# Conditioning of gates and second norm in a decoder layer: loads one visit ahead, products of a visit in one run

## The chip, the core and the metric

One core of a Trainium2 chip runs the whole program. The metric is the device time of one execution in microseconds (us), the median of the runs. TensorE is called PE, VectorE DVE, ScalarE ACT, GpSimd POOL and SyncE SP; SP does no arithmetic here, its queue issues most DMAs.

## The reference, cut to what matters

One layer of a hybrid autoregressive decoder, for two request groups with shared weights: a prompt of 256 positions and 8 sequences of 4 positions. N = 288 columns of activations run through every projection; the model width is 2048. Nine condition vectors (one for the prompt, eight for the sequences) give the six modulation vectors of the layer.

```python
mod = silu(c) @ w_ada + b_ada                      # 9 x 12288
sh1, sc1, g1, sh2, sc2, g2 = split(mod, 6)         # parts 0 to 5
h = rmsnorm(x, norm1) * (1 + sc1) + sh1
u_pool, z, xbc, dt = split(h @ w_in)
mix = concat([pool_mixer(u_pool), ssd_mixer(z, xbc, dt)]) @ w_out
x = x + g1 * mix                                   # needs part 2
h2 = rmsnorm(x, norm2) * (1 + sc2) + sh2           # needs parts 3 and 4
gate, val = split(h2 @ w_up)
x = x + g2 * ((silu(conv(gate)) * val) @ w_down)   # needs part 5
y = rmsnorm(x, norm_f)
```

The mixers are a causal pooling mixer (512 columns) and a chunked state-space scan (1536 columns), whose output is multiplied by silu(z) and normalized. "The gates and the second norm" of the title are parts 2, 3 and 4: the gate `g1` of the first residual and the shift and scale of the second norm. The change touches how these three parts are computed, and nothing of what is computed.

## The kernel before, in words

**Large products.** Every projection is taken in three products per 128 x 128 tile of weights (`mm3`, L299 to 302): the weights and the activations are both split into a high part of type fp32r and a remainder, and high x high, high x remainder and remainder x high are summed in PSUM. Activations have 288 columns. The 128 x 1024 block of weights that one load brings (8 tiles, so 24 products) is split by ACT (the cast into `whi`, L286) and DVE (the remainder `wlo`, L288).

**One ring for all weights.** `load` (L267 is its DMA) takes the next tile `raw` of a ring and issues its DMA of 512 KB on SP's queue. The ring has 8 buffers in the stages below (`RAW1`), one more from the sixth column tile of the output projection on; `whi` and `wlo` have 2 each until then, 4 afterwards. A DMA into a buffer can start once the last reader of that buffer is done. A buffer of projection weights is read by its cast and remainder; a buffer of conditioning weights is read by PE itself, as the moving operand of the products. SP issues in the order of the program's text, and a DMA that waits for its buffer holds up those behind it.

**Stages in order of time**: the modulated norm and the first projection's blocks 0 to 5 (tile `xbc`, parts 0 and 1 of the conditioning woven in between); the last block of that projection (`bi == 6`, 28 column tiles of 4 k each, preceded by the small projection `dt` and its elementwise stage `dt_stage`); the z stage (`uz_units`: the remaining columns for z and the pooling mixer, tiles `mm_uz`); the output projection (`mm_out`, `project_units`); the gated feed-forward (`mm_up`, `mm_gate`, `mm_val`, `mm_down`). The scan's small products run woven into the last block and the z stage.

**Conditioning of parts 2, 3 and 4.** `ada_part_units` makes one part. For each of the 16 k it loads two blocks of 128 x 1024 weights and calls `ada_mm` (its product is L329), which issues two products per block: 128 x 32 conditions against 128 x 512 weights, on four column tiles of PE (`tile_position`), so that four products run side by side. With `AY = 2` the generator pauses after every second k. What lies between two pauses is called a visit here: 2 k, 4 loads, 8 products; 8 visits make a part and 24 the three. After its last k the sum goes through ACT (`ada_sb`), four transposes (`ada_tr`) and four additions of the bias into the table `ada`.

The generators of parts 2, 3 and 4 are chained into `adas`, and the main program pulls visits from it at given rates: one every 4 column tiles of the last `xbc` block (`RA1`), one every 5 steps of two k in the z stage (`RA2`), two behind it (`TA`), one every two column tiles of the output projection and one each from column tile 10 on (`ADA_OUT`), and what is left after column tile 13. Part 5 is a call of its own, `adag2`, with one k a visit, between the output projection and the first gate tiles.

**What sets the order.** Instructions are recorded in the order of the text. On PE, ACT and DVE a scheduler may move them, by readiness and by the engine's work; `tc.high_priority()` lets an instruction go ahead of others that are ready, and `tc.keep_in_program_order(i)` ties an instruction to the one recorded before it. The order is fixed when the program is built: on the chip each engine waits at its next instruction, even if a later one could run. The first stage, up to the first norm, is put in order by `in_order`. In the conditioning of parts 0 and 1 (`ada_group_units`) all products of a visit but the first are tied in this way already, and they are taken from the visit's last load backwards, so that PE waits only once, at the first product.

**Around the change.** In the last block, after the products of `dt`: `late_states` issues three DMAs on SP's queue and one copy on POOL; then `dt_stage` runs on DVE and ACT. At the end of the z stage `y_norm` makes the norm of the scan's output (column sums and a broadcast on PE, the multiplication `zy` at L902 on DVE and POOL), and the operands of the output projection are formed by ACT and DVE (L1062 to 1071).

Of the kernel before, what the change touches and what calls it, by code (L numbers as in the profile page):

```python
# [12 lines left out]
F32 = mybir.dt.float32  # L13
# [5 lines left out]
P = 128  # L19
D = 2048  # L20
KT = D // P
# [30 lines left out]
AY = 2  # L52
# [26 lines left out]
def _xbc_chunks(bi):  # L79
    (k0, gk), (a, b) = BLOCKS[bi]  # L80
    mper = RAWC // (gk * P)
    cuts = [a, *([4, 8] if bi == 0 else []), *range(a + (12 if bi == 0 else mper), b, mper), b]
    return [(list(range(k0, k0 + gk)), list(range(m, n))) for m, n in zip(cuts, cuts[1:])]
# [78 lines left out]
def kernel(ctx: ExitStack, tc, ins, outs):  # L162
    nc = tc.nc
# [6 lines left out]
    pa = ctx.enter_context(tc.tile_pool(name="pa", bufs=1, space=PSUM))  # L170
# [29 lines left out]
    ada = kp.tile([P, 6, KT, NC9], F32, name="ada")  # L200
    amul = kp.tile([P, 2, KT, NC9], F32, name="amul")
    bada = early[:, V_BADA:V_BADA + 96].rearrange("p (a k) -> p a k", a=6)
    sc_c = kp.tile([P, KT, 32], F32, name="sc_c")
# [3 lines left out]
    @contextmanager  # L207
    def in_order(*engines):

        traced = nc.cur_bb.bb.instructions  # L210
        n0 = len(traced)
        yield
        prev = {}
        for i in list(traced[n0:]):
            if i.engine in engines:
                if i.engine in prev:
                    tc.add_manual_dep(i, prev[i.engine].name, mybir.DependencyInfo(
                        mybir.DependencyClass.NoSync, mybir.DependencyReason.DATA), reason="in_order")
                prev[i.engine] = i
# [44 lines left out]
    def load(key):  # L264
        off, cols = S.items[key]
        t = wp[0].tile([P, RAWC], F32, tag="raw", name="raw_" + "_".join(map(str, key)))
        nc.sync.dma_start(t[:, :cols], wflat[off:off + P * cols].rearrange("(p n) -> p n", p=P))  # L267
        return t

    queue = deque(_need_order())  # L270
    ahead = {}
    nloads = [0]

    def top_up():

        while queue and nloads[0] - min((n for n, _ in ahead.values()), default=nloads[0]) < RAW0 + RAW1:
            key = queue.popleft()
            ahead[key] = (nloads[0], load(key))
            nloads[0] += 1

    def fetch(key):
        return ahead.pop(key)[1]

    def split_steps(raw, a, n, name):
        hi = wp[0].tile([P, RAWC], F32R, tag="whi", name="whi_" + name)
        yield nc.scalar.copy(hi[:, :n], raw[:, a:a + n])  # L286
        lo = wp[0].tile([P, RAWC], F32R, tag="wlo", name="wlo_" + name)
        yield hi, lo, nc.vector.tensor_tensor(lo[:, :n], raw[:, a:a + n], hi[:, :n].bitcast(F32), ALU.subtract)  # L288

    def split(raw, a, n, name, urgent=True, pin=False):  # L290
        with tc.high_priority() if urgent else nullcontext():
            cast, (hi, lo, rest) = split_steps(raw, a, n, name)
        if pin:
            tc.keep_in_program_order(cast)
            tc.keep_in_program_order(rest)
        return hi, lo

    def mm3(ps, whi, wlo, c, bh, bl, first, last, n=P):
        w = slice(c * n, c * n + n)  # L299
        nc.tensor.matmul(ps, whi[:, w], bh, start=first, stop=False)  # L300
        nc.tensor.matmul(ps, whi[:, w], bl, start=False, stop=False)  # L301
        nc.tensor.matmul(ps, wlo[:, w], bh, start=False, stop=last)  # L302
# [23 lines left out]
    def ada_mm(ps, raw, k, c0, nb, js):  # L326
        for j in js:
            c = c0 + (j - js[0]) * nb
            nc.tensor.matmul(ps[32 * j:32 * j + 32, :nb], sc_c[:, k, :], raw[:, c:c + nb],  # L329
                             start=(k == 0), stop=(k == KT - 1), tile_position=(0, 32 * j))  # L330

    def ada_sb(ps, nb, name, r=P):
        asb = kp.tile([P, 512], F32, tag="asb", name="asb_" + name)
        nc.scalar.copy(asb[0:r, :nb], ps[0:r, :nb])
        return asb

    def ada_tr(asb, nb, name, r=P):
        pt = aux("adat_" + name)
        for i in range(nb // P):
            nc.tensor.transpose(pt[:, i * r:(i + 1) * r], asb[0:r, i * P:(i + 1) * P], ident[0:r, 0:r])  # L340
        return pt

    def ada_scale(which, part, norm, k0, gk):
        nc.vector.scalar_tensor_tensor(
            out=amul[:, which, k0:k0 + gk, :], in0=ada[:, part, k0:k0 + gk, :], scalar=1.0,
            in1=norm[:, k0:k0 + gk].unsqueeze(2).to_broadcast([P, gk, NC9]),
            op0=ALU.add, op1=ALU.mult)

    def ada_group_units(gi):
# [49 lines left out]
            nc.vector.tensor_tensor(o, src, b.unsqueeze(3).to_broadcast([P, 2, nj // 2, NC9]), ALU.add)  # L399
        ada_scale(0, 1, early[:, V_N1:V_N1 + KT], k0, gk)  # L400

    def ada_part_units(part, ay=1):
        ps = pa.tile([P, 512], F32, tag="ada", name=f"adap{part}")
        for k in range(KT):
            raws = [load(("adap", part, k, h)) for h in range(2)]
            for h in range(2):
                ada_mm(ps, raws[h], k, 0, 512, range(2 * h, 2 * h + 2))
            if k % ay == ay - 1:
                yield
        asb = ada_sb(ps, 512, f"p{part}")  # L410
        yield
        pt = ada_tr(asb, 512, f"p{part}")
        for i in range(4):
            o = ada[:, part].rearrange("p (j i) c -> p j i c", j=4)[:, :, i, :]
            b = bada[:, part].rearrange("p (j i) -> p j i", j=4)[:, :, i]
            src = pt[:, i * P:(i + 1) * P].rearrange("p (j c) -> p j c", j=4)[:, :, 0:NC9]
            nc.vector.tensor_tensor(o, src, b.unsqueeze(2).to_broadcast([P, 4, NC9]), ALU.add)
        if part == 4:
            ada_scale(1, 4, vec[:, V_N2:V_N2 + KT], 0, KT)
        yield  # L420
# [105 lines left out]
    def late_loads():  # L526
        nc.vector.tensor_copy(selr, seli)
        nc.vector.tensor_scalar(csr, vec[:, K_TRI:K_TRI + N], 0.0, None, ALU.mult)

    def late_states():  # L530
        nc.sync.dma_start(poolw, ins["pool_w"])
        n = XT * NB * 3
        st = sx[0].tile([P, n + 4 * NB * 15], F32, name="st")
        nc.sync.dma_start(st, ins["st"])
        stc.append(st[:, 0:n].rearrange("p (g m b l) -> p g m b l", g=4, m=5, b=NB))
        nc.gpsimd.tensor_copy(ups.rearrange("p m b l -> p (m b) l")[:, :, 0:15],
                              st[:, n:].rearrange("p (m l) -> p m l", l=15))
# [369 lines left out]
    def chain(*gens):  # L907
        for gn in gens:
            yield from gn

    adas = chain(*(ada_part_units(p, AY) for p in (2, 3, 4)))
    with in_order(*(e.engine for e in (nc.tensor, nc.scalar, nc.vector))):
        nc.scalar.activation(warm, sc_c[:, 0, 0:1], AF.Sqrt, scale=0.0)
        warm_pe(WU[0])
# [1 line left out]
        for q in range(4):  # L916
# [5 lines left out]
            for i in range(4):  # L922
                nc.tensor.matmul(ssum[32 * i:32 * i + 32, :N], ones[:, 0:32], sq[:, i, :],
                                 start=(q == 0), stop=(q == 3), tile_position=(0, 32 * i))
# [16 lines left out]
        parts = [split_steps(t, 0, len(ms) * P, f"xbc0_{i}") for i, (t, (_, ms)) in  # L941
                 enumerate(zip(first, _xbc_chunks(0)))]
# [47 lines left out]
    def pull(gn, rate):  # L990

        credit[id(gn)] = credit.get(id(gn), 0.0) + rate
        while credit[id(gn)] >= 1:
            credit[id(gn)] -= 1
            next(gn, None)

    nloads[0] = len(first) + KT // 4
    for bi in range(len(BLOCKS)):
        last = bi + 1 == len(BLOCKS)
        top_up()  # L1000
        if last:

            wp[0].drop(w0)
            w0_ctx.close()
            sx[0] = mx_ctx.enter_context(tc.tile_pool(name="sx", bufs=1, reuse_waits="tile"))
            hi, lo = split(load(("dt",)), 0, KT * NH, "dt")
            ps = pm.tile([P, 512], F32, tag="mm", name="mm_dt")
            for k in range(KT):
                mm3(ps[0:NH, :N], hi, lo, k, xhi[0][k], xlo[0][k], k == 0, k == KT - 1, NH)
            late_states()  # L1010
            dt_stage(ps)
        elif bi == 4:
            nc.sync.dma_start(vec, ins["vec"])
        elif bi == 5:
            late_loads()
        for i, m in enumerate(xbc_units(bi)):
            if not last:
                top_up()
                if bi == 0 and i in (3, 7, 13):
                    ci = {3: 2, 7: 3, 13: 4}[i]  # L1020
                    ready["xbc", 0, ci] = split(fetch(("xbc", 0, ci)), 0, len(_xbc_chunks(0)[ci][1]) * P,
                                                f"xbc0_{ci}", pin=True)
                if i in VIS[bi]:
                    next(nxt)
                    top_up()
            else:
                pull(back, 0.5 if m < 20 else RB1) if m >= 9 else None
                pull(adas, RA1 / AY)

    late = {}  # L1030
    n = 0
# [31 lines left out]
    for g in range(4):  # L1063
        for t in range(3):
            k = 4 + 3 * g + t
# [353 lines left out]
```

## Time and profile before

| what | value |
|---|---|
| median of 3 runs | 1358.91 us (1358.83 to 1359.32) |
| span of the profiled execution | 1356.6 us, 2.3 us under the median |
| PE busy | 1343.0 us, 99% |
| DVE, ACT, POOL busy | 810.8 us (60%), 579.2 us (43%), 222.1 us (16%) |
| conditioning parts 2 to 4 on PE | between 195 and 475 us of the span |
| read from memory | 309.78 MB, 236 GB/s over the span with what is written |

The profile shows one execution. Its span is what the engines and queues were seen to do; what lies outside of it (2.3 us against the median) is not in the trace. A row of the timeline has the start, the length, the engine, the line in the code, the operation, the tile written and the tiles read, the shapes and the count. Products of PE overlap: a large product is listed with 0.29 us, and the steps between their starts are shorter. A product of the conditioning counts as two records. "Idle before" names the time in which the engine had nothing running and what ended it. A line such as `PE mm_out L301 <- DVE mixl L1068: 0.4, 1, 0.4` says that PE's product waited for DVE: total us, number of waits, the longest. In the view of the DMA issues the time to landing runs from the moment that the queue has issued the DMA to the last byte's arrival.

### The profile page before, as it was taken

The page shows a single profiled execution, that of the slowest core. Times are in us where ns is not written, and L with a number is a line of the kernel's source. Part 1 is how long each engine was busy: PE and PEld are TensorE (multiplying, and loading weights), DVE is VectorE, ACT ScalarE, POOL GpSimd, SP SyncE. Part 2 cuts the span into 40 slices and gives each one's busy share as a digit, 9 for nine tenths or more (in the row PEclk, how much of TensorE's full clock was granted, in tenths as well). Part 3 has the DMA queues.
Part 4 walks back from the last instruction along what each step waited for, and adds up shares of the span by engine and source line. Part 5 has one row for each costly group of instructions (what it writes and reads, how often), then busy time and mean ns, then how long its engine had stood idle before and what let it go on. Part 6 is the DMA issues. An engine that isn't in the chain of part 4 may idle for free.

```text
span 1356.6 us, 26243 instructions
## 1 busy us (share of the span) xinstructions
PE 1343.0 (99%) x10557; PEld 1247.6 (92%) x10557; DVE 810.8 (60%) x1349; ACT 579.2 (43%) x910; POOL 222.1 (16%) x433
## 2 busy tenths in 40 slices
PE   9999999999999999999999999999999999999997
PEld 8889988777779889999999999999999999999997
DVE  5675568678564448645565455656554556566553
ACT  5243234587643335534443334443433334434452
POOL 0000002123221213111221001312220012222221
PEclk9999999999999999999999999999999999999999
DMA  9999768877988877787555555555555555565531
GB/s 374 405 408 363 253 218 326 333 259 289 335 298 332 314 261 260 238 303 262 185 181 185 165 179 184 197 193 181 187 177 167 186 189 190 189 204 190 182 119 70
DMA packets 97481, 323.18 MB, mean 238 GB/s; under 512 B 10768, under 2 KB 19920, under 8 KB 97360
## 3 DMA queue, kind: packets, MB, share of 16 engines
q1 hardware_dynamic: 93600, 310.79, 64.6%
q0 software_dynamic: 3184, 9.69, 1.9%
q8 instruction: 82, 1.34, 0.4%
q10 hardware_dynamic: 576, 1.03, 0.2%
q14 instruction: 39, 0.32, 0.1%
HBM read 309.78 MB, written 10.39 MB: 236 GB/s over the span
## 4 chain that ended last, share of the span: by engine, by line
PE 96%; DVE 2%; DMA 1%; ACT 0%; issue 0%; SPq 0%; POOL 0%; DVEq 0%; POOLq 0%; ACTq 0%
PE mm_down L301 7%; PE mm_down L300 7%; PE mm_down L302 7%; PE mm_val L301 6%; PE mm_gate L301 6%; PE mm_gate L300 6%; PE mm_val L302 6%; PE mm_gate L302 6%; PE mm_val L300 6%; PE xbc L300 5%; PE adap L329 5%; PE xbc L301 4%; PE xbc L302 4%; PE mm_out L300 3%; PE mm_out L301 3%; PE mm_out L302 2%
## 5 line engine op out<-in xcount | busy, mean ns | idle before, releaser
L301 PE MATMUL mm_down<-al,whi_down 128*128 128x288 f32 x688 | 202.5, 294 | 0.0
L300 PE MATMUL mm_down<-ah,whi_down 128*128 128x288 f32 x688 | 202.4, 294 | 0.0
L302 PE MATMUL mm_down<-ah,wlo_down 128*128 128x288 f32 x688 | 202.0, 294 | 0.0
L301 PE MATMUL mm_gate<-h2l,whi_gate 128*128 128x288 f32 x640 | 188.8, 295 | 0.0
L301 PE MATMUL mm_val<-h2l,whi_val 128*128 128x288 f32 x640 | 188.8, 295 | 0.0
L302 PE MATMUL mm_val<-h2h,wlo_val 128*128 128x288 f32 x640 | 188.7, 295 | 0.0
L302 PE MATMUL mm_gate<-h2h,wlo_gate 128*128 128x288 f32 x640 | 188.6, 295 | 0.0
L300 PE MATMUL mm_gate<-h2h,whi_gate 128*128 128x288 f32 x640 | 188.5, 294 | 0.0
L300 PE MATMUL mm_val<-h2h,whi_val 128*128 128x288 f32 x640 | 187.7, 293 | 0.0
L288 DVE TENSOR_TENSOR wlo_gate<-raw_gate,whi_gate 128x1024 fp32r<-128x1024 f32 x80 | 97.9, 1226 | 136.4 <-ACT whi_gate L286 134.3
L288 DVE TENSOR_TENSOR wlo_down<-raw_down,whi_down 128x1024 fp32r<-128x1024 f32 x96 | 108.2, 1127 | 116.0 <-ACT whi_down L286 116.0
L286 ACT CAST whi_down<-raw_down 128x1024 fp32r<-128x1024 f32 x96 | 92.4, 962 | 167.3 <-PE mm_down L301 117.9
L286 ACT CAST whi_gate<-raw_gate 128x1024 fp32r<-128x1024 f32 x80 | 83.9, 1051 | 161.0 <-PE mm_gate L301 65.4
L286 ACT CAST whi_val<-raw_val 128x1024 fp32r<-128x1024 f32 x80 | 84.1, 1051 | 123.1 <-issue 98.6
L300 PE MATMUL xbc<-h1h,whi_xbc 128*128 128x288 f32 x448 | 133.5, 301 | 0.8 <-ACT h1h L450 0.7
L301 PE MATMUL xbc<-h1l,whi_xbc 128*128 128x288 f32 x448 | 132.0, 296 | 0.0
L302 PE MATMUL xbc<-h1h,wlo_xbc 128*128 128x288 f32 x448 | 130.1, 296 | 0.0
L300 PEld LDWEIGHTS mm_down<-ah,whi_down 128*128 128x128 f32 x688 | 129.2, 188 | 0.0
L301 PEld LDWEIGHTS mm_down<-al,whi_down 128*128 128x128 f32 x688 | 129.1, 188 | 0.0
L302 PEld LDWEIGHTS mm_down<-ah,wlo_down 128*128 128x128 f32 x688 | 129.0, 188 | 0.0
L300 PEld LDWEIGHTS mm_gate<-h2h,whi_gate 128*128 128x128 f32 x640 | 120.3, 188 | 5.0 <-ACT ah L1184 3.4
L300 PEld LDWEIGHTS mm_val<-h2h,whi_val 128*128 128x128 f32 x640 | 120.3, 188 | 0.0
(325 smaller groups left out, 2978.4 us busy)
## 6 DMA issues: line engine op xcount, KB each, us to landing
raw_adap<-wflat SPq DMA_DIRECT2D x128, 512.0 KB, 5.8
raw_gate<-wflat SPq DMA_DIRECT2D x80, 512.0 KB, 3.5
raw_val<-wflat SPq DMA_DIRECT2D x80, 512.0 KB, 3.7
raw_ada<-wflat SPq DMA_DIRECT2D x64, 512.0 KB, 9.7
raw_xbc<-wflat SPq DMA_DIRECT2D x50, 512.0 KB, 9.5
raw_down<-wflat SPq DMA_DIRECT2D x48, 512.0 KB, 3.5
raw_out<-wflat SPq DMA_DIRECT2D x32, 512.0 KB, 7.2
raw_down<-wflat SPq DMA_DIRECT2D x32, 384.0 KB, 3.0
```

Source lines behind the costliest of these rows:

```text
L286: yield nc.scalar.copy(hi[:, :n], raw[:, a:a + n])
L288: yield hi, lo, nc.vector.tensor_tensor(lo[:, :n], raw[:, a:a + n], hi[:, :n].bitcast(F32), ALU.subtract)
L300: nc.tensor.matmul(ps, whi[:, w], bh, start=first, stop=False)
L301: nc.tensor.matmul(ps, whi[:, w], bl, start=False, stop=False)
L302: nc.tensor.matmul(ps, wlo[:, w], bh, start=False, stop=last)
L329: nc.tensor.matmul(ps[32 * j:32 * j + 32, :nb], sc_c[:, k, :], raw[:, c:c + nb], start=(k == 0), stop=(k == KT - 1), tile_position=(0, 32 ...
```

## The change

`adas` is made by one new generator, `ada_visits`, in place of the chain of three `ada_part_units`:

- *Loads.* The four loads of a visit are recorded right after the products of the visit before. The first visit's loads are recorded by an additional `next(adas)` in the last `xbc` block, between `late_states` and `dt_stage`. The number of visits pulled at each place of the text stays.
- *Products.* The products of a visit are taken from the last loaded block backwards. The first of them is free to be scheduled as before; the other seven have high priority and are tied to the one before. As the order within a visit is turned round, the sum of a part starts with the last k of its first visit and ends with the first k of its last.
- *The end of a part* (copy, transposes, bias) moves unchanged into `ada_finish`, which `ada_part_units` calls too. Part 5 goes on using `ada_part_units`.

```diff
+    def ada_visits(parts, ay):
+
+        plan = [(part, k) for part in parts for k in range(0, KT, ay)]
+
+        def chunks(v):
+            part, k0 = plan[v]
+            return [(k, h, load(("adap", part, k, h))) for k in range(k0, k0 + ay) for h in range(2)]
+
+        ahead = chunks(0)
+        yield
+        for v, (part, k0) in enumerate(plan):
+            if k0 == 0:
+                ps = pa.tile([P, 512], F32, tag="ada", name=f"adap{part}")
+            n = 0
+            for k, h, raw in ahead[::-1]:
+                for j in (2 * h, 2 * h + 1):
+                    with tc.high_priority() if n else nullcontext():
+                        i = nc.tensor.matmul(ps[32 * j:32 * j + 32, :], sc_c[:, k, :],
+                                             raw[:, 512 * (j % 2):512 * (j % 2) + 512], start=k == ay - 1,
+                                             stop=k == KT - ay, tile_position=(0, 32 * j))
+                    if n:
+                        tc.keep_in_program_order(i)
+                    n += 1
+            if v + 1 < len(plan):
+                ahead = chunks(v + 1)
+            yield
+            if k0 + ay == KT:
+                yield from ada_finish(ps, part)
+
     def ada_part_units(part, ay=1):
         ps = pa.tile([P, 512], F32, tag="ada", name=f"adap{part}")
...
             if k % ay == ay - 1:
                 yield
+        yield from ada_finish(ps, part)
+
+    def ada_finish(ps, part):
         asb = ada_sb(ps, 512, f"p{part}")
         yield
...
-    adas = chain(*(ada_part_units(p, AY) for p in (2, 3, 4)))
+    adas = ada_visits((2, 3, 4), AY)
...
             late_states()
+            next(adas)
             dt_stage(ps)
```

## The prediction

> **What bounds the kernel now.** I read the page first, for the engine that sets the end, then the windows of the stage that the change touches, then the PE timeline around single visits, then the waits of PE and of SP's queue, and last the chain of waits at the change from the z stage to the output projection.
>
> ```profile
> span 1356.6 us, 26243 instructions
> ...
> PE 1343.0 (99%) x10557; PEld 1247.6 (92%) x10557; DVE 810.8 (60%) x1349; ACT 579.2 (43%) x910; POOL 222.1 (16%) x433
> ...
> PE 96%; DVE 2%; DMA 1%; ACT 0%; issue 0%; SPq 0%; POOL 0%; DVEq 0%; POOLq 0%; ACTq 0%
> ```
>
> PE is busy for 99% of the span and carries 96% of the chain that ended last. A microsecond of PE work that goes is gained, and one in which PE waits is lost, one to one, except in the 2% where the chain runs over DVE. The products of conditioning parts 2, 3 and 4 (tile `adap`) lie between 195 and 475 us; part 5 comes later and its code stays.
>
> ```profile
> core 0: us, PE busy (x) PEld busy (x) ACT busy (x), PEclk, DMA share, GB/s
> 195.00:475.00 280.00, 53.65 (x384) 10.74 (x384) 1.73 (x3) 1.00 0.83 308
> ```
>
> This is the row of the windows for tile `adap`: 53.65 us of PE for 384 records, two a product, 24 visits of 8 products. The clock is granted in full; DMA runs at 0.83 of its time, so a load often queues here. A visit in one piece, a visit cut short, and a longer run look like this:
>
> ```profile
> 227.93 0.29 PE L302 MATMUL xbc<-h1h,wlo_xbc 128*128 128x288 f32 x1
> 228.15 1.92 PE L329 MATMUL adap<-raw_adap,sc_c 128*32 128x512 f32 x16
> 230.01 0.40 PE L300 MATMUL xbc<-h1h,whi_xbc 128*128 128x288 f32 x1
> 230.24 0.29 PE L301 MATMUL xbc<-h1l,whi_xbc 128*128 128x288 f32 x1
> 230.37 0.29 PE L300 MATMUL xbc<-h1h,whi_xbc 128*128 128x288 f32 x1
> ...
> 201.50 0.29 PE L302 MATMUL xbc<-h1h,wlo_xbc 128*128 128x288 f32 x1
> 201.73 1.04 PE L329 MATMUL adap<-raw_adap,sc_c 128*32 128x512 f32 x2
> 202.70 0.40 PE L300 MATMUL xbc<-h1h,whi_xbc 128*128 128x288 f32 x1
> 202.95 0.29 PE L301 MATMUL xbc<-h1l,whi_xbc 128*128 128x288 f32 x1
> ...
> 503.53 2.78 PE L329 MATMUL adap<-raw_adap,sc_c 128*32 128x512 f32 x22
> ```
>
> Columns: start, length, engine, line, operation, count. The large products follow each other every 0.13 us (230.24 to 230.37). From 227.93 to 230.24 are 2.31 us, of which two steps of 0.13 would have passed anyway: a whole visit costs 2.05. A single product (two records) costs 202.95 - 201.50 - 0.26 = 1.19. Eight products take 1.92, eleven 2.78: four run side by side as one wave, a further wave is 0.86, and each run pays 0.13 on top of its length (2.05 - 1.92) for entering and leaving.
>
> **Part 1: runs joined, a gain.** In the timeline the 24 visits of parts 2 to 4 form 32 runs; these are the first and the last:
>
> ```profile
> 198.09 1.92 PE L329 MATMUL adap<-raw_adap,sc_c 128*32 128x512 f32 x16
> ...
> 470.61 1.92 PE L329 MATMUL adap<-raw_adap,sc_c 128*32 128x512 f32 x16
> ```
>
> In the changed program's order they form 22: each visit is whole, and visits 0 and 1, and 21 and 22 (k = 10 to 13 of part 4), follow each other directly. Before: 53.65 + 32 x 0.13 = 57.8. After: 24 x 1.92 + 22 x 0.13 - 0.1 = 48.8. Gain **9.0 us**. The order also cuts the large products for other small groups (scan, transposes) 45 times instead of 52. By the visit's own switches, 2.05 - 1.86 = 0.2 (1.86 from its first product to the next large one's start, 228.15 to 230.01), that is 0 to 1.4; I take **0.6**, since some of these groups now only stand beside a visit.
>
> **Part 2: loads moved, two new waits.** No DMA is added; SP issues the same 96 loads of these parts, each four ahead of the weights that it stood behind. All tiles share a ring of 8 raw buffers, so I followed every weight load to the visit whose products free its buffer, and counted products on PE from there to the weight's first use. Before, the shortest distances are 55, 61 and 62. After, the last projection block (`xbc_6`) from its fifth load on keeps 62 to 97, but two places have 15: `xbc_6_2` behind visits 0 and 1, and `out_9_0` behind visits 21 and 22. Before, `xbc_6_2` did not wait for a visit at all. What such a load costs:
>
> ```profile
> 199.19 0.33 SPq L267 DMA_DIRECT2D raw_adap<-wflat  x1
> ...
> DMA to landing us min/median/max: 3.4/5.8/11.4
> ```
>
> ```profile
> L286 ACT CAST whi_out<-raw_out 128x1024 fp32r<-128x1024 f32 x32 | 33.2, 1046 | 29.5 <-PE mm_out L301 19.2 <-DMA raw_out<-wflat 9.5 <-ACT asb_p L334 0.8
> L288 DVE TENSOR_TENSOR wlo_out<-raw_out,whi_out 128x1024 fp32r<-128x1024 f32 x32 | 38.8, 1222 | 31.1 <-ACT whi_out L286 31.1
> ```
>
> The load at 199.19 waits for visit 0's first wave, which began at 198.09: a buffer comes free 1.1 us into a run. Landing takes 3.4 us where nothing queues (the minimum; I use 3.5) and 5.8 in the middle. Cast 1.05, remainder 1.22.
>
> At visits 0 and 1: free at 1.1, landed 4.6, cast 5.65 us after the run's start. PE has both visits done at 1.92 + 2 x 0.86 = 3.64, with the switch 3.75: it waits 1.9. The products with `wlo` need 5.65 + 1.22 = 6.9, and PE has by then 4 products (0.53) to pass the time: another 0.6. Sum **2.5**. Behind PE nothing else can go, its order is fixed; DVE and ACT idle with it. The next load, `xbc_6_3`, with 37 products ahead of it, comes in right behind the first and is covered by the same wait. At visits 21 and 22 the same, with 2 products instead of 4 ahead of the first `wlo`: 1.9 + 0.9 = **2.8**. Bounds for both together, by landing at 3.4 and at 5.8: 5.1 to 9.9. I take the low side, for DMA has run dry at both places: at the second one all loads ahead of it were released long before.
>
> The Trainium skill, DMA: Bandwidth & Descriptors (Anatomy of one DMA), fits a DMA as 2.0 us plus bytes / 436e3, on the software path. For 524288 bytes that gives 3.2 as an estimate; the trace's minimum is 3.4. By the page's figure the two waits would be 0.3 each less.
>
> In the z stage the distances fall to 55, 58, 42 (`uz_14_1`) and 33 (`uz_1_1`). The last two include small scan products of up to 0.3 us beside the 0.13 ones, about 5 to 6 us, against 3.5 + 1.05 for the cast: cover just there. I put **0.3** (0 to 3.5, if they land by the median).
>
> **Part 3: the stage in which PE had nothing better to do.**
>
> ```profile
> 374.79 1.90 PE L329 MATMUL adap<-raw_adap,sc_c 128*32 128x512 f32 x10
> 377.39 0.75 PE L881 MATMUL pool<-pout,poolw 128*128 128x288 f32 x2 [0.69 <-DVE pout L876]
> 378.51 1.06 PE L329 MATMUL adap<-raw_adap,sc_c 128*32 128x512 f32 x6
> 380.63 1.06 PE L329 MATMUL adap<-raw_adap,sc_c 128*32 128x512 f32 x8
> 383.98 1.05 PE L329 MATMUL adap<-raw_adap,sc_c 128*32 128x512 f32 x2
> 388.72 1.06 PE L329 MATMUL adap<-raw_adap,sc_c 128*32 128x512 f32 x6
> ```
>
> ```profile
> 371.54 3.98 DVE zy L902 x3
> ...
> 378.42 2.27 DVE wlo_out L288 x2
> ...
> 382.10 0.40 PE mm_out L301
> ```
>
> Two visits lie here in five runs, and joining them frees 6.13 + 5 x 0.13 - 2 x 2.05 = 2.7 us of part 1's gain. But from 371.54 the chain of waits runs over DVE (norm of the scan's output, operands of the projection, split of its first weights), 10.6 us to 382.10, and the change takes nothing off DVE. PE already idled there for the pool row's 0.69 and the next:
>
> ```profile
> PE mm_out L301 <- DVE mixl L1068: 0.4, 1, 0.4
> ```
>
> After, PE has the normalizer's broadcast earlier in its order by one visit, yet fewer fragments to fill with. What is freed turns into waits for `wlo_out` and `mixl`: between 0 (the chain starts early enough) and the whole 2.7. I take **2.1**, near the upper end, as the row for DVE is nearly unbroken and PE at 382.10 waits in before too.
>
> Covers at no price: the waiting first product of a visit now finds data loaded a visit ago, and the waits of PE for `raw_adap` go into part 1. The three short loads of the initial states on SP's queue move by 4 to 6 places; they are used many products later. If that cover went, the scan's `yo` products would wait at most one landing.
>
> **Sum.** -9.0 - 0.6 + 2.5 + 2.8 + 0.3 + 2.1 = **-1.9 us** on a span of 1356.6. The median of the runs, 1358.91, lies 2.3 above that span and the change touches nothing outside it: 1358.91 - 1.9 = **1357.0**. About 0.2% (2.7 us) is what a measurement of this kernel can tell from no change.
>
> **Rivals.**
>
> *Slower: the late weights.* All weights with a distance of 58 or less land by the row's median, 5.8, not 3.5. The two places with 15 then cost 2.3 more each, the ones with 42 and 33 about 2.3 each, the other two about 0.8 each (55 products and a wave are 8 us, 5.8 + 1.05 + 1.22 are 8.1, and a queue of states' loads stands ahead): 4.6 + 4.6 + 1.6 = 10.8, in place of nothing; +8.9, 1367.8. Each microsecond of landing costs 4 us, so it turns the sign from 0.5 us on, and passes 0.2% at 1.15 us. For it: DMA's 0.83, and this row, where a weight's cast starts only as it lands:
>
> ```profile
> L286 ACT CAST whi_xbc<-raw_xbc 128x1024 fp32r<-128x1024 f32 x12 | 12.6, 1046 | 23.7 <-DVE dttmp L561 7.1 <-DVE xde L732 7.1 <-DMA raw_xbc<-wflat 6.4
> ```
>
> Against it: a median comes from loads with three others ahead, and the loads at the two places are the first of their burst. Chance 0.22.
>
> *Clearly faster.* DVE's stretch follows the earlier broadcast and gives nothing back, the scan's switches count whole, and loads land at their minimum: -9.0 - 1.4 + 5.1 = -5.3, 1353.6. For it: the norm starts one visit earlier in PE's order. Against it: 0.69 and 0.4 of idling there already. Chance 0.26.
>
> *The clock.* PE is at full clock in the row of the windows, and its longest wait there is 0.7 us; the new ones are 1.9 at a time. If such a wait halved the clock for as long as the wait and its neighbours last, some 3.4 us at half speed at each of two places lose 1.7 each: -1.9 + 3.4 = +1.5, 1360.4. The rule behind it is the Trainium skill's, TensorE: Matmul & The Clock Gate (Part 1): an idle window of about 3.4 us halves the clock, and as long a busy one restores it. By that rule 1.9 is too short, and only a load that lands 1.5 us late would do; no row of this trace has such a wait. Chance 0.06.
>
> That the change would not do what it says is excluded by the order: every visit is one run there.
>
> **How the numbers follow.** Forecast 0.46, with 1355.2 to 1358.8 of its own (DVE's share from 0.7 to 2.7, landings 3.4 to 3.9). About 0.08 of it lies below 1356.2. Faster: 0.08 + 0.24 of the fast rival = 0.32. Slower: 0.20 of the late weights, whose mildest form stays inside 1361.6. Same: 0.48, the clock among it. The range takes most of the fast rival and the mild half of the late weights (landings up to 4.9: 1.4 x 4 - 1.9 = +3.7 and so 1362.6), and leaves out 0.2: 1354.0 to 1362.6.
>
> **What would show it.** Right: in the windows of tile `adap` for parts 2 to 4, 22 runs and some 46 us of PE; two waits of PE for the cast of 1.5 to 2.5 us, near 202 and near 450 us, each followed by a shorter one for the remainder; around 375 to 390 us PE's waits for DVE over 2 us in sum. Wrong: waits of PE for a cast at other visits (late weights), no wait for `mixl` or `wlo_out` (faster), a granted clock below 1.00 between 195 and 475 (clock), or a main stream whose steps are not 0.13.

## The result: slower by 0.2%, with executions up to 7 us apart

| kernel | executions | median us | lowest to highest | mean granted clock |
|---|---|---|---|---|
| before, beside the changed | 7 | 1359.02 | 1358.71 to 1359.97 | |
| changed | 7 | 1363.18 | 1358.21 to 1365.11 | 0.9951 |
| changed, once more | 11 | 1361.83 | 1360.75 to 1363.14 | 0.9953 |
| before, beside that | 33 | 1358.61 | 1358.41 to 1359.77 | 0.9975 |

The ratio to before, taken of the mean times, is 1.0023 (95% interval 1.0013 to 1.0033), and 1.0024 (1.0015 to 1.0034) the second time. The medians differ by 4.2 and 3.2 us. The last column is the mean over the executions of the clock granted to PE; the tail behind the last product, where PE is idle, takes it below 1 in every kernel.

The profile of the changed kernel shows its quickest execution, 1358.21. Its page:

```profile
span 1356.2 us, 26220 instructions
...
PE 1334.9 (98%) x10557; PEld 1246.6 (92%) x10557; DVE 813.1 (60%) x1349; ACT 579.6 (43%) x910; POOL 220.6 (16%) x433
...
PE 94%; DVE 3%; DMA 2%; ACT 0%; issue 0%; SPq 0%; POOL 0%; DVEq 0%; ACTq 0%; POOLq 0%
```

The windows row for tile `adap`, as in the prediction, and PE's waits by what they waited for (total us, times, longest):

```profile
195.00:475.00 280.00, 45.73 (x384) 10.32 (x384) 1.75 (x3) 1.00 0.84 311
```

```profile
PE mm_out L300 <- ACT whi_out L286: 2.3, 1, 2.3
PE xbc L300 <- ACT whi_xbc L286: 2.1, 1, 2.1
PE mm_out L302 <- DVE wlo_out L288: 1.1, 2, 0.7
...
PE xbc L302 <- DVE wlo_xbc L288: 1.0, 2, 0.6
PE mm_out L301 <- DVE mixl L1101: 0.8, 1, 0.8
...
PE mm_uz L302 <- DVE wlo_uz L288: 0.4, 1, 0.4
```

PE works 1343.0 - 1334.9 = 8.1 us less, and it is idle for 7.7 us more (21.3 instead of 13.6 outside its work): 0.4 us are left of the gain. The two new waits stand where they were forecast. The chain of waits shows the first of them from end to end:

```profile
198.33 1.02 PE adap L419 x8
199.36 3.50 DMA raw_xbc<-wflat
...
202.93 1.05 ACT whi_xbc L286
...
204.01 1.24 DVE wlo_xbc L288
...
205.29 0.40 PE xbc L302
```

The visit's first wave frees the buffer, the load takes 3.50, the cast 1.05, the remainder 1.24. So far this is the prediction's own account, and it ends at no change. The other executions of the same program take 2.7 to 6.9 us more, and their mean clock is 0.993 to 0.996 where this one has 0.998. What lowers it had to be found.

### The profile page after: what moved, and what is told of

It reads as the page before. It is cut to its first block, busy times and chain, and to the rows that moved or that the text cites. A ratio compares the mean times of both kernels' runs of the same rounds, so it can differ in the third digit from the quotient of the medians.

```text
span 1356.2 us, 26220 instructions
## 1 busy us (share of the span) xinstructions
PE 1334.9 (98%) x10557; PEld 1246.6 (92%) x10557; DVE 813.1 (60%) x1349; ACT 579.6 (43%) x910; POOL 220.6 (16%) x433
## 4 chain that ended last, share of the span: by engine, by line
PE 94%; DVE 3%; DMA 2%; ACT 0%; issue 0%; SPq 0%; POOL 0%; DVEq 0%; ACTq 0%; POOLq 0%
PE mm_down L301 7%; PE mm_down L300 7%; PE mm_down L302 7%; PE mm_val L301 6%; PE mm_gate L301 6%; PE mm_gate L300 6%; PE mm_val L302 6%; PE mm_gate L302 6%; PE mm_val L300 6%; PE xbc L300 5%; PE xbc L302 4%; PE xbc L301 4%; PE mm_out L301 3%; PE mm_out L302 2%; PE mm_out L300 2%; PE adap L419 2%
```

## The experiments

Two theories stand against each other in what follows. By the clock theory PE's new waits lower its clock in most executions. By the late-load theory some weights land later in most executions than in the first one.

**The changed kernel again, for a profile of a slower execution.**

> The changed kernel once more, for a profile of one of its slower executions (6 of its 7 lay 2.7 to 6.9 us above the first). Clock theory: the two waits of PE, 2.1 us near 202 and 2.3 us near 448, are there with the same lengths within 0.3 us, and behind one or both of them the granted clock is below 1.00 for 8 to 14 us in sum (a mean clock of 0.995 against 0.998 is 4 us of clock over the span); time 1361 to 1365. Late-load theory: the clock stays 1.00 outside the tail, and the two waits, or others for casts, are longer by 3 to 7 us in sum. If the profile catches an execution near 1358, the spread of the rounds is all that it tells.

Measured 1361.83, and the profile caught a span of 1359.7. These are windows of 3.41 us around the second wait (us, PE busy, granted clock, DMA share, GB/s), first of this execution, then of the quick one above:

```profile
446.42:449.83 3.41, 3.29 (x32) 1.00 0.34 129
449.83:453.24 3.41, 0.54 (x2) 1.00 1.01 400
453.24:456.66 3.42, 3.31 (x14) 0.50 1.02 414
456.66:460.07 3.41, 3.41 (x27) 1.00 1.03 414
```

```profile
446.04:449.46 3.42, 1.60 (x16) 1.00 0.91 321
449.46:452.87 3.41, 2.18 (x14) 1.00 1.01 408
452.87:456.28 3.41, 3.41 (x28) 1.00 1.02 416
```

The waits there are equally long in both (2.4 and 2.3 us for the cast, 0.7 for the remainder). The wait for the cast in the slower one:

```profile
PE mm_out L300 <- ACT whi_out L286: 2.4, 1, 2.4
```

In the slower execution they fall almost whole into one window, PE is busy for 0.54 us of it, and the next 3.41 us run at half clock: 14 records instead of 28. In the quick one the border lies in the middle of the wait; 1.60 and 2.18 us of work are left in the two windows, and the clock stays. The borders follow a grid that does not move with the program: in the quick execution I counted them back in steps of 3.413 us from the fall of clock behind the last product (the rise of the clock at its start lies 394 such steps earlier). So the clock theory holds in kind; of its numbers, "8 to 14 us below full clock" was one window of 3.41 in this execution (its clock 0.997), and by the mean clock (0.9975 - 0.9953 = 0.0022 of 1360 us, 3.0 us) it is 1.75 windows in the mean, each worth 1.7 us.

The clock is not all that sets these two executions apart: their spans differ by 3.5 us, of which the window at half clock is 1.7. Another 0.9 is one wait for `wlo_out` near 380 us (1.3 instead of 0.4).

**Both waits filled with work.** The program, its loads and its waits as changed; only PE is not idle:

```diff
+            if v in (1, 22):
+                for n in range(4 * 2):
+                    j = n % 4
+                    with tc.high_priority():
+                        i = nc.tensor.matmul(ps[32 * j:32 * j + 32, :], zero, vec[:, 0:512], start=False, stop=False,
+                                             tile_position=(0, 32 * j))
+                    tc.keep_in_program_order(i)
```

> Behind the two joined runs (visits 1 and 22) stand 8 further products each of a zero operand, which add nothing to the sums: 1.7 us in which PE works and would have waited. Loads and their waits are untouched. Clock theory: PE is never idle long there, so every execution is near 1358.2 (1357.5 to 1359.5), as the first of the changed kernel, though PE has 3.4 us more to do. Late-load theory: spread and median of the changed kernel, 1361 to 1365, as the weights land when they land.

Measured 1358.62 (11 executions, 1357.93 to 1359.27), ratio 0.9999 (0.999 to 1.0008), mean clock 0.9975, the same as before. PE has 3.4 us more to do, and the kernel is 3.2 us quicker than the unfilled one of the same chip. The windows at the second place now read:

```profile
446.43:449.84 3.41, 3.41 (x36) 1.00 0.81 290
449.84:453.25 3.41, 2.08 (x15) 1.00 0.97 393
```

The weights land as before: with 1.7 us filled, the waits for the two casts are 0.5 and 0.6 instead of 2.1 and 2.3. Late loads would not have been helped by this; that theory falls.

**Each place alone.** The same with `v in (1,)` and with `v in (22,)`.

> The filling products of zero stand behind visit 1 only; the wait of 2.3 us near 448 stays open. Clock theory: the granted clock falls for one window of 3.41 us in most executions, all of them near 450: a mean clock of 0.996 to 0.998 over the executions (one window is 0.00125) and a median between the change and the version filled at both places, 1359.5 to 1361. If the place near 202 alone did the harm: 1358.2 to 1359. If only the place near 448 does it: 1361.3 to 1362.5, as unfilled.

> The filling products stand behind visit 22 only; the waits of 2.1 and 0.6 us near 202 stay open. Clock theory with both places alike: 1359.5 to 1361, so that this gain and that of the other half add up to the 3.2 us of filling both. If the place near 448 alone did the harm: 1358.2 to 1359.

Measured 1359.81 with the first place filled and 1359.66 with the second, mean clocks 0.9959 and 0.9964. These ran on another chip, where the kernel before takes 1358.74 with a mean clock of 0.9977. With one place open the kernel is 1.1 or 0.9 us above the kernel before, with both open 3.2, with none 0.0, each on its own chip: the two places do like harm. The halves were expected to add up to the 3.2 us of filling both; they do not (filling saves 2.1 at the first place and 2.3 at the second), and why was not traced. The profile of each shows the clock fall at the place left open. With the second place filled it falls near 202:

```profile
202.58:206.00 3.42, 1.52 (x9) 1.00 1.02 407
206.00:209.41 3.41, 3.41 (x16) 0.50 1.03 417
```

With the first place filled it falls near 448, here for two windows in a row:

```profile
447.06:450.48 3.42, 1.22 (x12) 1.00 0.99 359
450.48:453.89 3.41, 2.79 (x10) 0.50 1.02 413
453.89:457.30 3.41, 3.41 (x16) 0.50 1.03 416
```

**Waits of known length.** To see what makes the clock fall, I put waits into the kernel before, in the down projection, where PE runs without a break: in every second column tile of its first two parts the next product waits until ACT has copied the unfinished sum 2 to 7 times.

> The kernel before, with 16 waits put into the first two parts of the down projection, 12 us apart, where PE otherwise never waits: in every second column tile, after 8 of its k, ACT copies the unfinished sum 2 to 7 times into a spare tile, and PE may go on when ACT has read it. With 0.39 us a copy and some 0.3 us to pass the word the waits are 1.1, 1.5, 1.9, 2.2, 2.6 and 3.0 us. Theory from the runs so far: time is cut into windows of 3.41 us; a window in which PE is busy for 1.5 us or less puts the next one at half clock, a window with 1.6 or more does not. Then waits below 1.8 us never lower the clock, those of 1.9 to 2.6 do so where they fall into one window (about half of them), those of 3.0 in three of four: 5 to 8 windows at half clock of 16, each 3.41 us, and none elsewhere. Rival, the clock falls only after a wholly idle window: none. Rival, it falls by the length of the wait alone: every wait above some length, none below. Time: 33 us of waits and 1.7 us for each window, 1397 to 1408.

Measured 1426.07 (2 executions). The copies took longer than I had put them at (waits of 1.1 to 3.9 us), so the time is out; what counts is which waits lowered the clock. Of 14 waits that ended with the copies, 8 brought one window at half clock and 6 none; at the other two places the woven-in updates of the states (`hs`) made PE wait too, and two windows in a row followed. No window at half clock lies elsewhere ahead of the tail. Three of the waits in the timeline:

```profile
844.96 0.40 PE L301 MATMUL mm_down<-ah,whi_down 128*128 128x288 f32 x1 [2.59 <-ACT gapt L1238]
...
1100.42 0.40 PE L301 MATMUL mm_down<-ah,whi_down 128*128 128x288 f32 x1 [3.02 <-ACT gapt L1238]
...
1131.16 0.40 PE L301 MATMUL mm_down<-ah,whi_down 128*128 128x288 f32 x1 [2.59 <-ACT gapt L1238]
```

and the windows on the grid, the one that holds most of the wait and the one behind it:

```profile
842.77:846.19 3.42, 1.23 (x9) 1.00 0.44 144
846.19:849.60 3.41, 3.41 (x16) 0.50 0.34 135
1098.77:1102.18 3.41, 1.75 (x13) 1.00 0.43 120
1102.18:1105.60 3.42, 3.42 (x28) 1.00 0.01 3
1129.49:1132.90 3.41, 1.74 (x13) 1.00 0.45 143
1132.90:1136.32 3.42, 3.42 (x28) 1.00 0.24 92
```

A wait of 2.59 us lowers the clock, another of 2.59 does not, and neither does one of 3.02, which a border cuts in two. What tells these apart is PE's work within a window of the grid. Over the profiles of all kernels here, from 20 us on to the tail, every window at full clock with 1.52 us of work or less was followed by one at half clock; of those with 1.60 or more only two were (1.76 at one of the `hs` places, and one of 3.14, below). No wholly idle window is needed, and the length of a wait alone does not tell.

**Nine raw buffers.** `RAW0, RAW1, RAW2 = 7, 9, 1`, where the change has 8, 8, 1, and the rest as it is.

> The change with nine raw buffers where it has eight (seven instead of eight in the early extra pool). xbc_6_2 and out_9_0 then stand behind an earlier user of their buffer. Both theories: the waits of 2.1 + 0.6 and 2.3 + 0.7 us are gone or below 0.5 each. Clock theory: the granted clock stays as before and the runs are tight, 1353 to 1354.5. Late-load theory: some later weights still come late in most executions, 1355 to 1360 with a spread over 2 us. If the buffers are not what these weights wait for: 1358 to 1365 as the change.

Measured 1360.61 (1359.55 to 1363.08), mean clock 0.9961: a miss of both theories' times. It lies in the range named for the case that the weights do not wait for the buffers, yet they did: the waits for the two casts are down to 0.6 and 0.5. But others have come up:

```profile
PE mm_out L301 <- DVE mixl L1101: 1.8, 1, 1.8
PE xbc L302 <- DVE wlo_xbc L288: 1.4, 2, 1.1
PE mm_uz L302 <- DVE wlo_uz L288: 1.2, 1, 1.2
PE mm_up L300 <- ACT h2h L482: 1.2, 1, 1.2
```

and the clock fell in a window that is nearly full by the profile's count:

```profile
211.88:215.29 3.41, 3.14 (x21) 1.00 1.02 411
215.29:218.70 3.41, 3.41 (x15) 0.50 1.03 412
```

In it stand the small products of `dt_stage` (24x24, 128x48, 32x24), some 0.35 us apart, each listed with 0.4 us. A product that stands alone is listed longer than it takes in a run (0.40 against a step of 0.13 for a large one), so the busy time of such a window overstates the work; that this is the whole reason was not tried. The two long waits became several shorter ones, most of them for DVE, and the time fell by 1.2 us only. Whether the smaller early pool cost something I did not separate.

**One half of the change each.** First the tying without the loads ahead: `ahead = chunks(v)` stands before the products of visit v, and the priming call records nothing.

> The change without its loads ahead: products of a visit tied and taken backwards, each visit's loads recorded right ahead of its products as before. 24 runs in one piece. No weight stands behind a visit with fewer products than before, so both waits should be missing. Clock theory and the sum of the prediction: the gain of joined runs, about 53.7 + 32 x 0.13 - 24 x 2.05 = 8.7, less some 2 to 4 us that turn into waits for DVE near 375: 1352 to 1354.5, tight. Rival: without the loads ahead the first product of a visit waits for its last load, which is why visits were cut: 24 visits at 0.2 to 0.5 us each bring it to 1357 to 1364.

Measured 1357.79 (1356.51 to 1358.61), ratio 0.9992 (0.9983 to 1.0001); 4.0 us under the changed kernel on the same chip, and above the 1352 to 1354.5 that were expected. Neither of the two waits for a cast is there, and the first products of the visits do not wait. Much of what it lacks shows in the stage behind the z stage, where PE now arrives earlier than DVE: waits of 1.2 and 1.9 us within some 4 us (0.7 and 0.4 before), and a window at half clock. The mean clock, 0.9958, is 2.3 us of the span below that of the kernel before.

```profile
PE pool L911 <- DVE pout L906: 2.1, 2, 1.2
PE mm_out L301 <- DVE mixl L1099: 1.9, 1, 1.9
```

```profile
374.47:377.88 3.41, 1.19 (x6) 1.00 0.99 339
377.88:381.29 3.41, 3.31 (x12) 0.50 1.02 414
```

Then the loads ahead without the tying: products in their old order, free to be cut.

> The other half of the change alone: loads one visit ahead, products neither tied nor turned round. The visits stand in 39 runs instead of 32 before and 22 in the change. By the prediction's prices: 7 runs more at 0.13 + some 0.5 us of a wave not shared cost about 4 to 5 us, the two waits for weights stay (5 to 6 us), and their clock with them (3): 1369 to 1374. If the loads ahead were what helps, and the tying did nothing: 1355 to 1359.

Measured 1382.01 (5 executions), ratio 1.0166 (1.0148 to 1.0184), further up than expected. Between 195 and 475 us PE is idle for 13 us (2.2 before):

```profile
195.00:475.00 280.00, 267.05 (x1976) 0.98 0.78 289
```

The weights wait at more places, in the z stage above all:

```profile
PE mm_uz L300 <- ACT whi_uz L286: 4.2, 3, 1.9
```

Four windows at half clock take 6.8 us. The 10.7 us of added idling and the clock make 17.5 of the 23.3 us by which it is slower than before; the rest was not traced. The loads ahead are the harmful half, and the tying covers for most of it. My account of why, not shown step by step: in a visit that is cut into pieces the last product comes later, so the buffers come free later.

**A version that beats both.** In the tied kernel the wait for `mixl` is DVE's order, not its amount of work: the pooling mixer's steps stand ahead of the operands' remainders. The twelve remainders (`mixl`) get high priority:

```diff
-            nc.vector.scalar_tensor_tensor(out=xlo[0][k], in0=zy[g][:, t, :], scalar=gv,
...
+            with tc.high_priority() if 3 * g + t < 12 else nullcontext():
+                nc.vector.scalar_tensor_tensor(out=xlo[0][k], in0=zy[g][:, t, :], scalar=gv,
...
```

> Tied products without loads ahead, and the twelve remainders of the output projection's operands (mixl) get high priority on DVE, so that they stand ahead of the pooling mixer's work. In the version without it PE had 1.2 + 1.9 us of waits between 373 and 378 and one window at half clock right there. Clock theory: the waits are shorter and further apart (0.5 to 1.5 each), the window is missing in most executions, and the time falls by its 1.7 us and up to 1 us of waits: 1354.8 to 1356.5. Rival: DVE has the same work to do, so the waits return at the pooling operands: 1357 to 1358.5.

Measured 1355.66 (11 executions, 1354.74 to 1356.53), ratio 0.9978 (0.9969 to 0.9986): 3.1 us under the kernel before. The mean clock is 0.9974, only 0.4 us of the span below the 0.9977 of the kernel before on this chip. It beats the tied kernel by 2.3 us, each held against the kernel before on its own chip, and by the mean clocks 1.9 of them are the clock. In the stage behind the z stage the longest wait is 1.1 us instead of 1.9:

```profile
PE mm_out L302 <- DVE wlo_out L288: 1.7, 2, 1.1
...
PE pool L911 <- DVE pout L906: 0.8, 1, 0.8
```

Its control, the same priority in the kernel before:

> The kernel before, with the twelve remainders of the output projection's operands at high priority on DVE and nothing else: the control for the version in which the products are tied and the remainders come first (1355.7). If the gain there came from the order on DVE alone, 1355 to 1356.5; if it takes the joined runs, which bring PE to this stage earlier, 1358 to 1359.5.

Measured 1360.45, ratio 1.0012 (1.0003 to 1.0021), above both ranges: by itself the new order on DVE costs 1.8 us. Its profile has a wait that the kernel before does not have:

```profile
PE mm_out L302 <- DVE wlo_out L288: 1.9, 1, 1.9
```

Of the two kernels tried, the new order pays only in the one whose tied products bring PE to this stage early.

## Why the prediction was wrong, point by point

- **Runs joined.** Right in the count: 22 runs, 45.73 us where 46 were forecast. Mis-sized in the switches: 9.6 us were to be saved in all, 1.9 of them by fewer switches (10 x 0.13 and 0.6). PE's busy time fell by 8.1, of which the row for `adap` has 7.9, so only 0.2 of the 1.9 is seen. Where the rest went was not traced.
- **The two waits.** Right in place, cause and size: 2.1 + 0.5 near 202 (forecast 1.9 + 0.6) and 2.3 + 0.7 near 448 (1.9 + 0.9), with a load of 3.50 where 3.5 was taken. The later weights came in time but for short waits (0.4 us for `wlo_uz`, 0.6 for a `wlo_xbc` near 226); the rival of the late weights did not happen.
- **The DVE stage.** Mis-sized: between 374 and 392 us PE's waits for DVE are 1.1 us before (0.7 for `pout`, 0.4 for `mixl`) and 1.2 after (0.8 for `mixl`, 0.4 for `wlo_out`), so of the 2.1 forecast next to nothing came there. The 0.7 for `pout` now lies near 343, and the short waits just named came up elsewhere.
- **The sum.** On the profiled executions -0.4 for a forecast of -1.9, and 1358.2 for 1357.0. The four waits of the forecast add up to 7.7 us, as much as PE was idle more; that is luck, as the one for DVE was 2 us too large and short waits elsewhere made up for it. The 1.5 us by which the sum is off lie in the first part, in the switches.
- **The clock** is the step that failed. It was a rival with a chance of 0.06, set aside because "1.9 is too short" for a window of 3.4, and the sum has nothing for it. Two things were wrong in that. I held each wait by itself against the window, though at both places a second wait follows within 0.6 to 0.8 us of work: 2.1 + 0.5 and 2.3 + 0.7 are 2.6 to 3.0 us of idling in a stretch of 3.4 to 3.6. And I took the Trainium skill's rule (TensorE: Matmul & The Clock Gate, Part 1) at its word, that an idle window of some 3.4 us is needed. The runs agree with this page of the Trainium skill that the windows have 3413 ns (3.41 here), run freely and that the clock then is one half (0.50 here); they differ on the point that mattered, as 1.52 us of work in a window did not keep the clock up. The price per place was right (1.7 us of clock), and 1.75 such windows an execution lead from -0.4 to +2.6; measured was +3.2 in the repeat and +4.2 the first time.

The first profile shows the quickest of seven executions, in which the grid happened to leave 1.60 us of work or more in every window between the start and the tail. By that luck it shows the forecast nearly right (1358.2 for 1357.0), while the range ended 0.6 us below the median of the seven.

## What to carry to other kernels

When an edit trades switching on PE for a wait of 2 us or more, price the wait twice: once as lost time, and once for the window of half clock that may follow (1.7 us each here); add up all idling that lies within 3.4 us, not each wait by itself. If executions of one program spread by several microseconds while its profile looks clean, look at the clock of each execution, and fill the wait with products of zero to test it. Loads issued early from a shared ring hold buffers that the next weights need: count the products between the step that frees a buffer and the first use of what comes into it.

## What the runs showed of the hardware

Windows at half clock are 3.41 us long, on a grid of their own, and a window in which PE was busy for 1.52 us or less, 45%, brought one; 1.60 to 1.75 us of large products did not. Listed busy time alone does not tell for small or lone products: a window with 3.14 us of it, products of 24 to 48 columns among large ones, was followed by half clock. How such products count was not tried.
